# The first half of the next mixer pass as a stream beside the last chunk's delta rule

## The chip, the core and the metric

The kernel runs on one core of a Trainium2 chip. The metric is the device time of one execution in microseconds. Lower is better. The engines are TensorE (PE; its weight loads are listed apart as PEld), VectorE (DVE), ScalarE (ACT), GpSimd (POOL) and SyncE (SP), which here only issues transfers.

## The reference

One layer over 1024 tokens of width 1024, in float32. The mixer's input projection feeds two groups of heads, and its output goes through cross attention and a layer of experts.

```python
h = rmsnorm(x)
qkv, z, a_in, b_in, xr, gate = split(h @ w_in)
q, k, v = split(silu(causal_dwconv(qkv)))          # 4 taps along the tokens
g    = -exp(a_log) * softplus(a_in + dt_bias)
beta = sigmoid(b_in)
# gated delta rule, 4 heads of 128:
#   S_t = exp(g_t) S_{t-1} (I - beta_t k_t k_t^T) + beta_t v_t k_t^T,  o_t = S_t q_t
y_gdn = rmsnorm(o) * silu(z)
y_lru = rg_lru(causal_dwconv(xr)) * gelu(gate)     # a linear recurrence along the tokens
x = x + concat(y_gdn, y_lru) @ w_out
x = x + cross_attention(rmsnorm(x), rmsnorm(mem))  # 4 heads, 256 memory tokens
# experts: per token and each of 8 heads the 16 best of 128 x 128 product keys
x = x + sum_e gate_e * v_e * gelu(u_e . rmsnorm(x))
out = rmsnorm(x)
```

## The kernel before

The tokens go through the mixer in four passes of 256 (`T`), each of two chunks of 128 (`NB` = 2). `mixer` (L414) does a pass:

- It transposes the normed x into `hT`, multiplies for the gates g and beta, and then makes 12 tiles of 128 columns for query, key and value (`proj_T`, L319, with a weight tile of 512 KB each), each followed by a convolution on ScalarE and VectorE (`conv`, L415). They are kept in `qkv`: columns 0 to 3 are queries, 4 to 7 keys, 8 to 11 values. Columns 4 to 11 also hold the x of the next pass once keys and values are done with.
- It starts a stream `side` (L472): the z projection, and the linear recurrence with its eight projection tiles.
- It runs the gated delta rule chunk by chunk. A chunk is one long chain: small products on TensorE, each followed by a copy or a product on ScalarE or VectorE, six levels of a block recursion among them. In the last chunk, when keys and values are read, it issues the load of the next pass's x (`load_x`, L607).
- When the recurrence and both chunks are through, it norms the next x in place (`norm_x`, L738), and multiplies by the output projection (`out`, L523), which takes the x of the pass plus that product as `x1`.

Only then does the next pass begin. The passes run in the loop of `mixed` (L1224).

Beside them runs `attended` (L1238): first the keys and values of the memory, then the attention units (128, 128, 256, 256 and 256 tokens; `attend`, L757). A unit needs the `x1` of its tokens. It ends with the product keys, 16 tiles of queries and a search for the 16 best on VectorE, and with `choose` (L846), a stream that selects the experts. After the mixer comes the stream `gated` (L1233) that writes a table of gates for the 512 tokens that go by all experts, and at the end the dense part (`dense`, L1016), TensorE work for these tokens. The other 512 tokens go by their experts' rows: 1024 steps (`step`, L1138), each a gather of 128 rows by GpSimd, issued a few steps ahead, and one VectorE instruction over 128 x 1024 that is pinned behind the VectorE instruction emitted before it. Half of the steps of a block use the u rows, the others the v rows. The steps that are left after the dense part are emitted behind it.

The order in which all this is emitted is made by a planner in the program (`together`, L1176). It holds an estimate of when each engine is through. Of the streams that are ready it takes the one of least rank, and at equal rank the one that had the least TensorE time for its share:

```python
c = min(ready, key=lambda x: (x.rank, x.had / x.share))
```

The mixer and its side have rank 1 and share 6. `attended` has rank 2 and share 1 until the memory's keys and values are made, then rank 0 until the first experts are chosen, then rank 1. The gates have rank 0. A stream that yields `None` lets another go first.

The steps of the row stream are put between TensorE's instructions, one for each `pe.pace` nanoseconds of TensorE's estimated time (`tick`, L115):

```python
while self.ns > self.pace and (not self.real or dve.at < self.at + SLACK and not late_row()):
    self.ns -= self.pace
    step()
```

The pace is 2800 in the first three passes, 3500 in the fourth and in the gates (`PACES`, `PACE_G`), 2250 in the dense part (`PACE_D`). `mixed` sets it when a pass begins. The tiles `X1` (x1), `hT`, `qkv` and the memory that row gathers share with the first pass's split operands exist once.

Of the kernel before, what the change touches and what calls it, by code (L numbers as in the profile page):

```python
# [22 lines left out]
D0 = T                      # the tokens that go by all experts; the others go by their experts' rows  # L23
# [26 lines left out]
def block_kernel(ctx: ExitStack, tc: tile.TileContext, a):  # L50
# [3 lines left out]
    written = {}                # by tile: when which part of it is written, by the estimate  # L54
# [17 lines left out]
    class Engine:  # L72
        """An engine, and an estimate of when it is through with what it got so far."""
# [25 lines left out]
    class Paced(Engine):  # L99
        """The tensor engine, with steps of the stream of rows put between its instructions."""  # L100
# [29 lines left out]
    early = gat.tile([128, NROW + 2, D], FR, name="rb")   # until the rows come  # L130
# [9 lines left out]
    # ---------------------------------------------------------------- constants  # L140
    identf = consts.tile([128, 128], F, name="identf")
    identb = fc.tile([128, 128], BF, name="identb")
    triu = fc.tile([128, 128], F, name="triu")          # [t, i] = t <= i
    ones = fc.tile([128, 128], F, name="ones")
    negm = fc.tile([128, 128], BF, name="negm")         # [j, i] = -1e30 where i < j
    iota16 = consts.tile([128, 16], BF, name="iota16")
    # masks of the block recursion: W = (T X) o (I - M_s); M_s[r, c] = 1 where r // s is odd
    # and c // s = r // s - 1 (the first one transposed)
# [53 lines left out]
    lpar = ld("lpar", (128, 4, 4))                          # conv_b, ba, bx, lambda  # L202
# [9 lines left out]
    # ---------------------------------------------------------------- helpers  # L212
    def rsqrt(v, n, name):
        """1/sqrt(v) for a positive [128, n] tile: a bit guess and Newton's steps."""
# [11 lines left out]
    def softplus(x, n, name):  # L226
        """max(x, 0) + log1p(exp(-|x|)), the log by its atanh series."""
# [24 lines left out]
    def wload(src):  # L252
        """A piece of weights: 1024 rows x 128 columns, [128, 8, 128]."""
        w = wp.tile([128, D], F, name="w", bufs=3)
        sp.dma_start(w, src)
        return c8(w)

    def norm(X, nb, Y, junk):
        """RMS of token-major tiles, to Y."""
# [9 lines left out]
    class Both:  # L269
        """Two tiles [128, 4, T] as one of 8."""  # L270
# [6 lines left out]
    class Pair:  # L277
        """A float32 operand as two float32r parts, for the time in which the gathered rows' memory
        is free; tmp: a place for [128, T] of products."""
# [3 lines left out]
    def low(i):  # L283
        """Memory of the rows, [128, 8, T]."""
        return early[:, 2 * i:2 * i + 2, :].rearrange("p s (c t) -> p (s c) t", c=D // T)

    def transposed(hT, Y, nb, wcol):
        """Token-major tiles to [d, chunk, tok], by the weights."""
# [30 lines left out]
    def proj_T(wname, j, hT, n):  # L319
        """[128 columns, n tokens] of the product with one 128-column tile of weights."""  # L320
# [17 lines left out]
    def proj(wname, j, lhs, nb, b0=0):  # L338
        """The token-major products [128 tokens, nb blocks, 128 columns]."""
# [18 lines left out]
    # ---------------------------------------------------------------- once: masks, gates' constants  # L358
# [18 lines left out]
    # ---------------------------------------------------------------- once: memory keys, values  # L377
# [26 lines left out]
    # ---------------------------------------------------------------- the mixer, T tokens  # L404
# [9 lines left out]
    def mixer(fp, t0, qkv):  # L414
        def conv(ps, ti, w, out, bias=0.0):  # L415
            """Causal 4-tap convolution along the tokens of one channel tile."""
# [10 lines left out]

        hT = fp.tile([128, 8, T], F, name="hT", bufs=1)
        if t0 < EARLY:
            hT = Pair(hT, low(0), tmp)  # L430
        yield from transposed(hT, blocks_of(qkv[:, 4:12, :]), NB, wmixc)

        # a, b: token-major
# [25 lines left out]
        # q, k, v: channel-major, convolved, silu  # L459
        for j in range(12):  # L460
# [9 lines left out]
        ready = set()  # L470

        def side():  # L472
            # z: token-major, 2 silu(z)
# [8 lines left out]
            # RG-LRU: channel-major  # L482
# [252 lines left out]
        while not ready >= {"y", *range(NB)}:  # L735
            yield None
# [594 lines left out]
```

## Time and profile before

| | |
|---|---|
| Time, median of 3 runs | 3305.86 us (3297.55 to 3307.26) |
| Span of the profiled execution | 3300.7 us |
| TensorE busy | 3053.8 us, 93% |
| VectorE busy | 2740.9 us, 83% |
| ScalarE busy | 1282.9 us, 39% |
| GpSimd busy | 1430.2 us, 43% |
| Mean granted clock of TensorE | 0.962 |

The profile is one execution; its span runs from the first to the last instruction. Of its own time no other number than the span is given, so it stands 5.2 us below the median of the runs. Times in the rows count from the span's start. A matmul in float32 is two instructions in the trace. The granted clock is a share of 2.4 GHz; the other level, 1.2 GHz, shows as 0.50. The stages below are cut where the timeline shows the first products of a chunk, of an output projection or of a pass: the second pass's chunks begin at 406 and 542 us, its output projection at 640; the third pass begins at 676, its chunks at 728 and 866; the fourth pass's chunks begin at 1066 and 1207; the mixer ends near 1359, the gates run to 1821, the dense part to 3287.

### The profile page before, as it was taken

The page shows a single profiled execution, that of the slowest core. Times are in us where ns is not written, and L with a number is a line of the kernel's source. Part 1 is how long each engine was busy: PE and PEld are TensorE (multiplying, and loading weights), DVE is VectorE, ACT ScalarE, POOL GpSimd, SP SyncE. Part 2 cuts the span into 40 slices and gives each one's busy share as a digit, 9 for nine tenths or more (in the row PEclk, how much of TensorE's full clock was granted, in tenths as well). Part 3 has the DMA queues.
Part 4 walks back from the last instruction along what each step waited for, and adds up shares of the span by engine and source line. Part 5 has one row for each costly group of instructions (what it writes and reads, how often), then busy time and mean ns, then how long its engine had stood idle before and what let it go on. Part 6 is the DMA issues. An engine that isn't in the chain of part 4 may idle for free.

```text
span 3300.7 us, 46517 instructions
## 1 busy us (share of the span) xinstructions
PE 3053.8 (93%) x16212; PEld 2638.8 (80%) x16212; DVE 2740.9 (83%) x5999; ACT 1282.9 (39%) x2694; POOL 1430.2 (43%) x1045
## 2 busy tenths in 40 slices
PE   7999997698999989999868799999999999999998
PEld 6888887677988878898868677888888878888886
DVE  7634776877787889887899798888999988899998
ACT  6833452236323632465358332222222222222222
POOL 0000233334433343333333475665666665656663
PEclk9999998899999999999868899999999999999999
DMA  4346778688887678778888788999998999899995
GB/s 170 111 145 210 251 279 309 228 290 291 297 298 284 232 259 320 270 265 282 303 279 234 289 326 328 335 335 335 336 333 323 331 337 332 325 345 327 340 333 197
DMA packets 321547, 941.66 MB, mean 285 GB/s; under 512 B 28912, under 2 KB 108832, under 8 KB 319264
## 3 DMA queue, kind: packets, MB, share of 16 engines
q0 software_dynamic: 148048, 538.04, 46.2%
q1 hardware_dynamic: 107216, 367.08, 30.5%
q10 hardware_dynamic: 66048, 33.56, 3.6%
q8 instruction: 128, 2.10, 0.2%
q14 instruction: 107, 0.88, 0.1%
HBM read 894.53 MB, written 44.04 MB: 284 GB/s over the span
## 4 chain that ended last, share of the span: by engine, by line
PE 56%; DVE 14%; DMA 10%; issue 9%; POOL 7%; ACT 4%; SPq 0%; POOLq 0%; ACTq 0%; DVEq 0%
PE pj L106 17%; PE dh L106 15%; PE po L106 14%; PE gd L106 7%; POOL rb L1130 7%; DVE rb L82 4%; DMA rb<-in_u,idx 4%; DVE oh L82 2%; PE sc L106 1%; DMA w<-in_pwq 1%; PE tp L111 1%; DMA gd<-stage 1%; DMA w<-in_wout 1%; DVE cy L82 1%; ACT L82 1%
## 5 line engine op out<-in xcount | busy, mean ns | idle before, releaser
L1130 POOL DMA_INDIRECT rb<-in_u,idx x512 | 682.3, 1333 | 1128.2 <-DVE rb L82 509.6
L1130 POOL DMA_INDIRECT rb<-in_v,idx x512 | 739.1, 1444 | 702.8 <-DVE rb L82 487.8
L82 DVE SCALAR_TENSOR_TENSOR rb<-rb 128x1024 f32<-128x1024 f32 x512 | 614.4, 1220 | 97.8 <-DMA rb<-in_u,idx 97.5
L82 DVE SCALAR_TENSOR_TENSOR rb<-rb,ga 128x1024 f32<-128x1024 f32 x512 | 655.6, 1280 | 12.5 <-DMA rb<-in_v,idx 6.1
L106 PE MATMUL pj<-hT,w 128*128 128x256 f32 (+1 forms) x2880 | 592.5, 358 | 18.0 <-DMA w<-in_pwq 12.8
L106 PEld LDWEIGHTS pj<-hT,w 128*128 128x128 f32 x2880 | 493.9, 196 | 75.8 <-DMA w<-in_pwq 13.7
L106 PE MATMUL dh<-hT_h,uh 128*128 128x512 f32 x1024 | 407.5, 398 | 17.8 <-ACT dg L82 17.1
L106 PE MATMUL po<-vh,dah 128*128 128x512 f32 x1024 | 404.7, 395 | 8.9 <-DVE acc L82 7.6
L106 PE MATMUL dh<-hT_l,uh 128*128 128x512 f32 x1024 | 406.4, 397 | 0.0
L106 PE MATMUL dh<-hT_h,ul 128*128 128x512 f32 x1024 | 406.3, 397 | 0.0
L106 PE MATMUL po<-vh,dal 128*128 128x512 f32 x1024 | 405.1, 396 | 0.4 <-DVE dal L82 0.4
L106 PE MATMUL po<-vl,dah 128*128 128x512 f32 x1024 | 405.1, 396 | 0.0
L82 ACT CAST uh<-ur 128x1024 fp32r<-128x1024 f32 x128 | 134.7, 1052 | 551.8 <-PE dh L106 363.5
L106 PE MATMUL gd<-ohg,oh 128*128 128x128 f32 x1024 | 254.7, 409 | 47.2 <-ACT ohg L82 28.6
L106 PEld LDWEIGHTS gd<-ohg,oh 128*128 128x128 f32 x1024 | 245.9, 328 | 56.3 <-ACT ohg L82 42.1
L106 PEld LDWEIGHTS dh<-hT_h,uh 128*128 128x128 f32 x1024 | 193.4, 189 | 65.8 <-ACT dg L82 18.0
L106 PEld LDWEIGHTS po<-vh,dah 128*128 128x128 f32 x1024 | 192.1, 188 | 57.8 <-DVE acc L82 9.3
L106 PEld LDWEIGHTS dh<-hT_h,ul 128*128 128x128 f32 x1024 | 193.1, 189 | 47.1
L106 PEld LDWEIGHTS dh<-hT_l,uh 128*128 128x128 f32 x1024 | 193.4, 189 | 46.5
L106 PEld LDWEIGHTS po<-vl,dah 128*128 128x128 f32 x1024 | 192.2, 188 | 47.2
L106 PEld LDWEIGHTS po<-vh,dal 128*128 128x128 f32 x1024 | 192.2, 188 | 47.0 <-DVE dal L82 0.8
L82 ACT CAST dah<-dg 128x512 fp32r<-128x512 f32 x128 | 79.5, 621 | 301.0 <-DVE dg L82 301.0
(338 smaller groups left out, 4836.2 us busy)
## 6 DMA issues: line engine op xcount, KB each, us to landing
ur<-in_ut SPq DMA_DIRECT2D x128, 512.0 KB
vr<-in_v SPq DMA_DIRECT2D x128, 512.0 KB
w<-in_wA SPq DMA_DIRECT2D x80, 512.0 KB
w<-in_pwq SPq DMA_DIRECT2D x80, 512.0 KB
gd<-stage ACTq DMA_DIRECT2D x32, 1024.0 KB
G<-gd SPq DMA_DIRECT2D x16, 2048.0 KB
w<-in_wout SPq DMA_DIRECT2D x40, 512.0 KB
w<-in_wq SPq DMA_DIRECT2D x40, 512.0 KB
```

What stands on the lines that cost most here:

```text
L82: r = call(*args, **kw)
L106: self.engine.matmul(out, l, r, **kw)
L111: self.engine.transpose(out, i, ident)
L1130: pool.indirect_dma_start(out=t, out_offset=None, in_=a[ph], in_offset=bass.IndirectOffsetOnAxis(ap=B["idx"][:, k:k + 1], axis=0))
```

## The change

`mixer` is cut into `heads` (norm of x, transposes, g and beta, the 12 tiles and the start of `side`) and `delta` (the delta rule and the output projection). `heads` of the next pass is started as a stream of the mixer's rank and share right behind the load of x in the last chunk. It first waits until the pass's recurrence is through, sets the pace of its pass, norms x (with `hT` as scratch in place of `zs`) and makes the key and value tiles; it makes the query tiles only when the output projection of the pass before is finished, because that reads the query columns as y. `delta` of the next pass follows its `heads`. Nothing that is computed changes. Lines of comments that the diff also drops are left out here.

```diff
-    def mixer(fp, t0, qkv):
+    class Pass:
+
+        def __init__(self, t0):
+            self.t0, self.ready, self.x1 = t0, set(), []
+
+        def finished(self):
+            return self.t0 in done and (self.t0 > 0 or 128 in done)
+
+    def heads(fp, P, prev, qkv):
+
+        t0, ready = P.t0, P.ready
+
...
+        while prev and "y" not in prev.ready:
+            yield None
+        pe.pace = PACES[t0 // T]
         hT = fp.tile([128, 8, T], F, name="hT", bufs=1)
+        if prev:
+            X = blocks_of(qkv[:, 4:12, :])
+            norm(X, NB, X, hT[:, 0:D // T, :].rearrange("p c t -> p (c t)"))
+            yield list(X)
         if t0 < EARLY:
             hT = Pair(hT, low(0), tmp)
         yield from transposed(hT, blocks_of(qkv[:, 4:12, :]), NB, wmixc)
...
-        for j in range(12):
+        for j in (4, 5, 6, 7, 8, 9, 10, 11, 0, 1, 2, 3):
+            while j == 0 and prev and not prev.finished():
+                yield None
             ps = yield from proj_T("wA", j, hT, T)
...
-        ready = set()
+        P.g, P.beta, P.zs, P.yl = g, beta, zs, yl
...
         yield Stream(side(), RANK[2], SHARE[2])
 
-        y, x1 = Both(qkv[:, 0:4, :], yl), []
+    def delta(fp, P, qkv, after):
+
+        t0, ready, x1 = P.t0, P.ready, P.x1
+        g, beta, zs, yl = P.g, P.beta, P.zs, P.yl
+        y = Both(qkv[:, 0:4, :], yl)
...
             if b == NB - 1 and t0 + T < S:
-                load_x(qkv, t0 + T)             # keys and values of this pass are done with
+                load_x(qkv, t0 + T)
+                yield Stream(after(), RANK[1], SHARE[0])
             yield L_STEP
...
-        while not ready >= {"y", *range(NB)}:
-            yield None
-        if t0 + T < S:
-            norm_x(fp, qkv)
         yield from out(0 if t0 else 1, NB)
-        while t0 not in done:
+        while not P.finished():
             yield None
...
     def mixed():
-        """The mixers, then the gates of the passes that take all experts."""
-        for i in range(NP):
-            pe.pace = PACES[i]
-            yield from mixer(fp, i * T, qkv)
+
+        def chain(i, prev):
+            P = Pass(i * T)
+            yield from heads(fp, P, prev, qkv)
+            yield from delta(fp, P, qkv, lambda: chain(i + 1, P))
+            if i == NP - 1:
+                over.add(0)
+
+        over = set()
+        yield Stream(chain(0, None), RANK[1], SHARE[0])
+        while not over:
+            yield None
         mix.close()
```

## Rows read from the trace of the kernel before

**Rows 1.** The page, its first part: busy time, share of the span, instructions.

```profile
PE 3053.8 (93%) x16212; PEld 2638.8 (80%) x16212; DVE 2740.9 (83%) x5999; ACT 1282.9 (39%) x2694; POOL 1430.2 (43%) x1045
```

**Rows 2.** Windows by stage: length, engines' busy time (instructions), granted clock, DMA share, GB/s.

```profile
406.00:542.00 136.00, 116.23 (x781) 106.99 (x780) 98.98 (x256) 72.71 (x190) 55.17 (x47) 0.92 0.82 289
542.00:640.00 98.00, 67.98 (x504) 64.60 (x502) 80.67 (x320) 19.77 (x48) 26.16 (x25) 0.86 0.73 251
640.00:676.00 36.00, 28.38 (x209) 27.62 (x209) 24.15 (x58) 5.42 (x8) 17.95 (x15) 0.83 0.80 291
676.00:728.00 52.00, 50.98 (x239) 40.31 (x239) 41.24 (x122) 21.48 (x55) 15.22 (x15) 0.99 0.79 273
728.00:866.00 138.00, 127.86 (x769) 113.03 (x768) 106.95 (x233) 82.21 (x212) 59.67 (x51) 0.99 0.81 286
866.00:990.00 124.00, 115.28 (x767) 106.69 (x766) 99.31 (x305) 25.75 (x59) 49.85 (x43) 0.97 0.87 307
1066.00:1207.00 141.00, 126.94 (x752) 112.35 (x750) 122.54 (x393) 85.17 (x210) 50.76 (x41) 0.98 0.71 246
1207.00:1359.00 152.00, 141.27 (x1004) 131.68 (x1003) 128.24 (x432) 38.37 (x89) 59.06 (x50) 0.99 0.84 300
1821.00:3287.00 1466.00, 1439.67 (x6143) 1155.49 (x6144) 1324.66 (x1587) 421.23 (x534) 885.14 (x577) 0.99 0.89 324
```

**Rows 3.** Waits of TensorE from 542 to 676 us: total, times, longest.

```profile
PE tp L111 <- DVE go L82: 11.9, 1, 11.9
```

**Rows 4.** Windows, ten microseconds near the second pass's end.

```profile
630.00:640.00 10.00, 1.23 (x4) 0.73 (x4) 9.76 (x35) 2.13 (x5) 4.07 (x3) 0.50 0.49 158
```

**Rows 5.** Groups by line and shape, whole span: busy us, mean ns, idle before.

```profile
L82 DVE SCALAR_TENSOR_TENSOR cy<-cbuf,hcw,cy 128x256 f32<-128x256 f32 x144 | 69.5, 483 | 3.5 <-ACT cy L82 0.6 <-issue 0.2
L82 DVE SCALAR_TENSOR_TENSOR qkv<-cth,cy 128x256 f32<-128x256 f32 x48 | 20.3, 422 | 8.9 <-ACT cth L82 8.5 <-issue 0.3
...
L82 DVE COPY cbuf<-hist 128x3 f32<-128x3 f32 x64 | 10.9, 174 | 1.1
...
L82 ACT ACTIVATE zs<-qkv 128x1024 f32<-128x1024 f32 x8 | 8.4, 1054 | 10.2 <-DVE go L82 7.6 <-DMA qkv<-in_x 2.6
```

**Rows 6.** Row steps (u, v) from 340 to 1014, to 1821 and to 3301 us.

```profile
L82 DVE SCALAR_TENSOR_TENSOR rb<-rb 128x1024 f32<-128x1024 f32 x128 | 153.7, 1220 | 23.5 <-DMA rb<-in_u,idx 23.4
L82 DVE SCALAR_TENSOR_TENSOR rb<-rb,ga 128x1024 f32<-128x1024 f32 x84 | 107.2, 1277 | 4.9 <-DMA rb<-in_v,idx 4.2
...
L82 DVE SCALAR_TENSOR_TENSOR rb<-rb 128x1024 f32<-128x1024 f32 x128 | 153.9, 1218 | 18.9 <-DMA rb<-in_u,idx 18.7
L82 DVE SCALAR_TENSOR_TENSOR rb<-rb,ga 128x1024 f32<-128x1024 f32 x104 | 132.7, 1276 | 0.6 <-DMA rb<-in_v,idx 0.4
...
L82 DVE SCALAR_TENSOR_TENSOR rb<-rb,ga 128x1024 f32<-128x1024 f32 x325 | 416.9, 1283 | 6.9 <-DMA rb<-in_v,idx 1.6
L82 DVE SCALAR_TENSOR_TENSOR rb<-rb 128x1024 f32<-128x1024 f32 x256 | 306.8, 1221 | 55.4 <-DMA rb<-in_u,idx 55.3
```

**Rows 7.** Timeline of VectorE at the end: start us, us, what.

```profile
3272.52 2.60 DVE L82 SCALAR_TENSOR_TENSOR rb<-rb,ga 128x1024 f32<-128x1024 f32 x2
...
3280.40 1.29 DVE L82 SCALAR_TENSOR_TENSOR rb<-rb,f_y,wfin 128x1024 f32<-128x1024 f32 x1
...
3287.58 0.69 DVE L82 TENSOR_TENSOR acc<-acc,po 128x512 f32<-128x512 f32 x1
...
3295.65 1.28 DVE L82 SCALAR_TENSOR_TENSOR acc<-acc,f_y,wfin 128x1024 f32<-128x1024 f32 x1
```

**Rows 8.** Groups from 1815 to 1837 us, where row steps ran unpaced.

```profile
L1130 POOL DMA_INDIRECT rb<-in_v,idx x12 | 15.5, 1294 | 8.8 <-DVE rb L82 4.2 <-issue 1.8 <-DVE gate L82 1.7
L82 DVE SCALAR_TENSOR_TENSOR rb<-rb,ga 128x1024 f32<-128x1024 f32 x11 | 14.2, 1287 | 1.8 <-DMA rb<-in_v,idx 1.6
```

**Rows 9.** One line's instructions: ns min/median/max, first and last start us.

```profile
L106 PE MATMUL pj<-hT,rb x640: 276/280/682, 17.2 to 228.6; 128*128 128x256 f32 x160
...
L1130 POOL DMA_INDIRECT rb<-in_u,idx x512: 932/1145/3137, 361.9 to 2949.1; - x171
```

## The prediction

> **What bounds the kernel now.** I read the page first, then the windows cut at the stages, then the waits inside the emptiest stage, then the groups by line for the fetched rows, and last the timeline of the end.
>
> The page shows TensorE busy for 93% of the span [rows 1]. That is a mean over two halves with different limits. From 1821 us on, the products with all experts run, and TensorE is busy for 1439.7 of 1466 us [rows 2]: nothing in the mixer touches that. Before it lies the front, where the mixer passes, the attention units, the selections and the gates share the engines. The reader is to see in its windows that most stretches are fed: between 728 and 1359 us (the four windows that I call fed) TensorE idles 10.1 of 138, 8.7 of 124, 14.1 of 141 and 10.7 of 152 us, 44 of 555 or 8%. Two stretches are worse: 406 to 542 us idles 19.8 us, and 542 to 676 us, the last chunk of the second pass with its output projection, idles 30.0 + 7.6 = 37.6 us, at a granted clock of 0.86 and 0.83 [rows 2]. There the attention stream has run out of work, because the next unit needs the output of this pass, and the longest wait of TensorE is for the delta rule's own VectorE result, 11.9 us [rows 3].
>
> There is a second clock that sets the end. 1024 steps work on gathered rows. The planner doles them out by its estimate of TensorE's time: one per 2.8 us, 3.5 us from the fourth pass on, 2.25 us in the dense part. In the trace 212 steps lie between 361.9 us, where the first gather is issued [rows 9], and 1014, 232 between 1014 and 1821, 581 after [rows 6], that is one per 3.08, 3.48 and 2.50 us. The last of them ends at 3275.1 us, and TensorE's last result is added at 3287.6 [rows 7]. So the rows end with a slack of 12.5 us, 5 steps. A front that ends earlier hands out fewer steps, and those that remain are emitted behind the last instruction of the dense part.
>
> **The change part by part.** No arithmetic is removed or added, and no transfer: the norm, 16 transposes, the gates' products and the 12 projection tiles with their convolutions move, tile loads on SP's queue with them.
>
> 1. What moves beside the last chunk. One projection tile is 16 instructions; 239 of them fill 51.0 us in 676 to 728 us [rows 2], 0.213 us each, 3.4 us a tile. Eight key and value tiles make 27 us, the gates' products another 3.4, transposes some 3: 34 us of TensorE a pass, three times. Four query tiles (14 us) stay behind the output projection. In the third and fourth pass this only changes places with attention work, since 866 to 990 us is fed already.
>
> 2. What it fills. If 406 to 676 us came to the 8% of the fed stretches, the idle falls from 57.4 to 21.6 us: 35 us (rounded down). That is the value I take. Upper bound: the clock too. The granted clock means 0.92, 0.86 and 0.83 there against 0.98 in the fed windows, and (0.98 less these) times the busy 116.2, 68.0 and 28.4 us is 7 + 8 + 4 = 19 us: 54 in all. Lower bound: VectorE. It is busy 80.7 of 98 us in 542 to 640, and 9.76 of 10 us from 630 to 640, where TensorE has 1.23 us of work and the 1.2 GHz level of the clock (0.50) [rows 2, 4]. The move brings eight convolutions of three taps at 0.483, one product of 0.422 and two copies of about 0.17 us, 2.2 us each [rows 5], and the gates' small operations, 18 us and more, onto the engine that the chunk already waits for. If only what fits without delay counts, 17.3 us are free in 542 to 640 and part of it lies between dependent operations: 10 us.
>
> By the Trainium skill, "Perfetto Trace Analysis", Identifying the Most-Contended Engine, matmul busy time is a poor measure and the busy share of weight loads the better one. The rows disagree on what is free: in 676 to 728 us loads fill only 40.3 us, but the matmuls stand 0.213 us apart without a gap. By the loads the idle is 71 us in 406 to 676 us and 16% in the fed stretches, so 26 us would be filled in place of 35, and the total would come out 7 us later.
>
> 3. Rows that start later. The stream that makes the memory's keys and values has rank 2, the mixer rank 1. In the first pass the moved work is always ready and goes ahead of it. Memory products end at 228.6 us now [rows 9]; 34 us of work in front of them delays the first attention unit, its selection and so the first gather by 33 us, since TensorE was nearly full there. 33 / 3.08 = 10.7 steps are not handed out. Between nothing, if that unit catches up, and this; I take all of it, as its rank cannot be evaded.
>
> 4. The pace of 3.5 us now begins with the fourth pass's first half, that is with the last chunk of the third (866 us) and no longer at 1014, and earlier by the lead that the mixer has gained (33 + 35 us). 216 us at 3.48 in place of 3.08 us a step lose 216 x 0.0373 = 8.1 steps.
>
> 5. A front 35 us shorter hands out up to 35 / 3.48 = 10 steps fewer; none, if the planner's clock never contained that idle. Between 362 and 1014 us the planner counted 212 x 2.8 = 594 of 652 us, so it missed about half of the time in which TensorE idled or ran slow. I take 5.
>
> 6. What missing steps cost. 10.7 + 8.1 + 5 less the slack of 5 is 19 steps behind the end. They follow the last VectorE instruction of the dense part, which now ends at 3296.9 us; after them come the square, root and product that took from 3275.1 to 3281.7 us, and the 3.7 us until the span ends [rows 7]: 6.5 us more than now, plus the steps. Where the pace let go, 11 steps stand in 22 us, the instruction on VectorE at 1.29 us and the gather on GpSimd at 1.29 and 1.8 / 12 = 0.15 us to issue [rows 8]. VectorE alone bounds a step by 1.29 us from below, that burst with all between it by 2.0 from above; I take 1.4, near GpSimd's own rate. 19 steps are 26.6 us, the give-back 33 us.
>
> 7. At nothing: the x load (it was issued at the same place before), the order of key, value and query tiles, the norm's other scratch tile. Their cover is the same as before, except under the third rival.
>
> Sum: the saving F less the give-back. With F free, the missing steps are 12.5 + 0.18 F, and the change of the time is 24 - 0.75 F. At F = 35 it is -2 us. The profiled execution has a span of 3300.7 us, 5.2 below the runs' median of 3305.9; 3298.5 plus this is 3304 us. Measurement can tell about 0.3%, 10 us, from no change.
>
> **The rivals.**
>
> Forecast, no change that can be told: F between 19 and 45 us. The fed windows, and 57 us of idle in reach, speak for it; chance 0.36, range 3295 to 3315.
>
> Faster: the gain reaches the clock as well, F = 54, change -16 us: 3290. The low clock stands only where TensorE starved [rows 2], which speaks for it. The same time results if the first rows come no later (10.7 steps, 15 us, are not lost: 3289). Against both speak VectorE's load and the ranks. Chance 0.32, from F = 45 on.
>
> Slower: VectorE is what the last chunk waits for. The convolutions lengthen the delta rule's chain instead of filling its holes; F = 10, the steps are lost all the same, +16 us: 3322. For it speak the 9.76 of 10 us [rows 4] and that wait [rows 3]; against it that the selection which fills VectorE there would move later along with the attention. It decides below F = 19. Chance 0.22.
>
> Slower too: the norm of x now stands on ScalarE right behind the load's issue. Up to now those squares waited 2.6 us in all for x [rows 5]. Two blocks are 1.05 MB; at the 251 GB/s of 542 to 640 us [rows 2] that is 4 us alone and 8 with half of it. Seven us in three passes would hold up the copies of the delta rule queued behind, F = 14: +13 us, 3319. Chance 0.10. Beside it stands the Trainium skill, "TensorE: Matmul & The Clock Gate", Architectural detail: VectorE and ScalarE take their queue strictly in order. The wait of 2.6 us neither bears that out nor speaks against it.
>
> That the change does nothing (the first half never overlaps, because the recurrence of the pass isn't through) I give no chance of its own: the recurrence's condition is met ahead of every last chunk in the timeline.
>
> **Numbers.** Faster 0.32, same 0.36, slower 0.32. Eight in ten reach from 3282 (F = 54 and half of the late rows not lost) to 3326.
>
> **What would show it.** Step 1: tiles of the next pass's keys between the delta rule's products of a last chunk. Step 2: the dense part begins near 1786 us, the stretch of the second pass's end at over 0.9 busy. Step 3: the memory products end near 260 and the first gather stands near 395 us. Steps 4 to 6: about 420 steps ahead of the dense part, and a block of some 19 row steps behind the last addition of the dense part. Wrong it would be if the front keeps its 1821 us, if the rows still end inside the dense part, or if VectorE's waits in the last chunks grow.

## The result and the profile after

| | before | after |
|---|---|---|
| median of the runs compared (4 and 4) | 3306.56 us | 3336.03 us |
| span of the profiled execution | 3300.7 us | 3328.8 us |
| products of the memory end | 228.6 us | 273.2 us |
| first gather of rows | 361.9 us | 426.3 us |
| dense part begins | 1821.0 us | 1789.1 us |
| row steps ahead of it, in it, behind it | 444, 581, 0 | 400, 585, 40 |
| last addition of the dense part | 3287.6 us | 3253.1 us |
| from there to the end of the span | 13.1 us | 75.7 us |

The changed kernel is slower by 0.9%: ratio 1.0088, with a 95% interval of [1.0064, 1.0112]. Between the two profiles the 28.1 us split into 31.9 us less in front of the dense part, 2.6 us less in it, and 62.6 us more behind it.

The page's busy times have hardly moved against [rows 1]:

```profile
PE 3046.5 (92%) x16212; PEld 2631.4 (79%) x16212; DVE 2741.3 (82%) x5999; ACT 1284.8 (39%) x2694; POOL 1406.4 (42%) x1045
```

What moved is shown by PE's timeline of the changed kernel inside the last chunk of the second pass. Between the products of the recursion (gd) now stand whole projection tiles of the third pass (pj<-hT,w, 128 x 256):

```profile
559.75 0.94 PE L106 MATMUL gd<-Xi,TT 128*128 128x128 f32 x7
560.53 3.62 PE L106 MATMUL pj<-hT,w 128*128 128x256 f32 x16
563.99 1.05 PE L106 MATMUL gd<-W,Y 128*128 128x128 f32 x8
564.88 3.62 PE L106 MATMUL pj<-hT,w 128*128 128x256 f32 x16
```

The windows of the changed kernel, columns as in [rows 2]. The first two hold the end of the second pass's delta rule and its output projection, the next four stretches of the third and fourth pass, then the dense part and what follows it:

```profile
520.00:640.00 120.00, 106.97 (x725) 95.09 (x723) 95.94 (x324) 38.65 (x103) 38.43 (x35) 0.93 0.85 296
640.00:682.00 42.00, 41.05 (x289) 38.80 (x289) 34.15 (x140) 6.89 (x13) 13.64 (x12) 0.96 0.77 269
682.00:852.00 170.00, 153.22 (x961) 137.26 (x960) 127.64 (x328) 89.62 (x220) 72.65 (x60) 0.96 0.80 281
852.00:975.00 123.00, 116.98 (x689) 102.50 (x687) 98.84 (x326) 40.60 (x98) 34.84 (x31) 0.99 0.79 263
1020.00:1161.00 141.00, 127.92 (x757) 113.53 (x756) 124.69 (x439) 81.31 (x198) 50.79 (x39) 0.99 0.69 236
1161.00:1325.00 164.00, 147.36 (x1031) 137.06 (x1030) 132.41 (x394) 34.55 (x77) 63.54 (x54) 0.95 0.84 297
1789.00:3253.00 1464.00, 1442.37 (x6144) 1157.65 (x6144) 1324.94 (x1574) 419.82 (x532) 876.26 (x587) 0.99 0.91 327
3253.00:3329.00 76.00, 0.00 (x0) 0.00 (x0) 64.37 (x105) 3.45 (x6) 39.04 (x34) 0.52 0.76 277
```

The hole of [rows 2] is filled: 14.0 us of idle in these 162 us, where 542 to 676 us had 37.6 us in 134, and the clock there is 0.93 and 0.96 for 0.86 and 0.83. TensorE's longest wait there is no longer for VectorE as in [rows 3], but for ScalarE:

```profile
PE tp L111 <- ACT hT L82: 5.2, 2, 4.9
PE tp L111 <- ACT qkv L82: 2.5, 2, 1.9
PE tp L111 <- DVE go L82: 1.9, 1, 1.9
```

The four later stretches idle 52.5 of 598 us, 9%, where the fed windows of before had 8%. And 76 us at the end have no product at all. VectorE's timeline there, against [rows 7]:

```profile
3253.14 0.68 DVE L82 TENSOR_TENSOR acc<-acc,po 128x512 f32<-128x512 f32 x1
...
3262.97 1.28 DVE L82 SCALAR_TENSOR_TENSOR acc<-acc,f_y,wfin 128x1024 f32<-128x1024 f32 x1
3264.17 10.52 DVE L82 SCALAR_TENSOR_TENSOR rb<-rb,ga 128x1024 f32<-128x1024 f32 x8
3275.26 3.92 DVE L82 SCALAR_TENSOR_TENSOR rb<-rb,ga 128x1024 f32<-128x1024 f32 x3 [0.56 <-DMA rb<-in_v,idx]
...
3309.36 10.53 DVE L82 SCALAR_TENSOR_TENSOR rb<-rb,ga 128x1024 f32<-128x1024 f32 x8 [1.33 <-DMA rb<-in_v,idx]
...
3323.42 1.28 DVE L82 SCALAR_TENSOR_TENSOR rb<-rb,f_y,wfin 128x1024 f32<-128x1024 f32 x1
```

From 3264.17 to 3319.89 us stand 39 row steps, 1.43 us each, and one before them. The numbers of steps are read from VectorE's groups, in front of the dense part (u and v rows) and behind it, against [rows 6]:

```profile
L82 DVE SCALAR_TENSOR_TENSOR rb<-rb 128x1024 f32<-128x1024 f32 x256 | 306.3, 1217 | 40.3 <-DMA rb<-in_u,idx 38.7 <-issue 1.7
L82 DVE SCALAR_TENSOR_TENSOR rb<-rb,ga 128x1024 f32<-128x1024 f32 x144 | 183.9, 1277 | 1.9 <-DMA rb<-in_v,idx 1.0
...
L82 DVE SCALAR_TENSOR_TENSOR rb<-rb,ga 128x1024 f32<-128x1024 f32 x40 | 51.4, 1284 | 5.6 <-DMA rb<-in_v,idx 4.5
```

The memory and the first gather, against [rows 9] (line L1151 was L1130):

```profile
L106 PE MATMUL pj<-hT,rb x640: 275/280/579, 16.5 to 273.2; 128*128 128x256 f32 x160
...
L1151 POOL DMA_INDIRECT rb<-in_u,idx x512: 932/1146/3097, 426.3 to 3026.3; - x171
```

### The profile page after: what moved, and what is told of

Same layout as the page of the kernel before. It is cut to its first block, busy times and chain, and to the rows that moved or that the text cites. A ratio compares the mean times of both kernels' runs of the same rounds, so it can differ in the third digit from the quotient of the medians.

```text
span 3328.8 us, 46501 instructions
## 1 busy us (share of the span) xinstructions
PE 3046.5 (92%) x16212; PEld 2631.4 (79%) x16212; DVE 2741.3 (82%) x5999; ACT 1284.8 (39%) x2694; POOL 1406.4 (42%) x1045
## 4 chain that ended last, share of the span: by engine, by line
PE 69%; DVE 14%; DMA 8%; ACT 4%; issue 4%; POOL 1%; SPq 0%; ACTq 0%; POOLq 0%; DVEq 0%
PE dh L106 21%; PE po L106 20%; PE pj L106 17%; PE gd L106 8%; DVE rb L82 4%; DMA rb<-in_u,idx 2%; PE sc L106 2%; PE tp L111 2%; DVE oh L82 1%; DMA w<-in_pwq 1%; DMA gd<-stage 1%; POOL rb L1151 1%; ACT L82 1%; DMA w<-in_wo 1%; DVE cy L82 1%
## 5 line engine op out<-in xcount | busy, mean ns | idle before, releaser
L1151 POOL DMA_INDIRECT rb<-in_u,idx x512 | 666.4, 1302 | 1231.2 <-DVE rb L82 579.7
L1151 POOL DMA_INDIRECT rb<-in_v,idx x512 | 731.2, 1428 | 672.3 <-DVE rb L82 443.8
```

The lines of the kernel that those rows point to most:

```text
L1151: pool.indirect_dma_start(out=t, out_offset=None, in_=a[ph], in_offset=bass.IndirectOffsetOnAxis(ap=B["idx"][:, k:k + 1], axis=0))
```

## The experiments

Two theories stood against each other. **A**: the front's 32 us are a gain of their own, and the steps that it no longer hands out can be won back. **B**: the front is shorter because it does 44 steps fewer; at equal numbers of steps it is as long as before. In the table the steps are counted in VectorE's rows, and the front ends with the first product of the dense part, in one profile of each kernel. Executions of one kernel spread by 5 to 26 us in total time, and the experiments ran on several chips; how far the front's end alone varies was not measured. So differences of single profiles under 10 us are not read, and those up to 20 only where several agree.

| kernel | steps in front | front ends, us | steps behind | ratio to before |
|---|---|---|---|---|
| before | 444 | 1821.0 | 0 | |
| after | 400 | 1789.1 | 40 | 1.0088 [1.0064, 1.0112] |
| e1 after, memory first | 414 | 1802.2 | 24 | 1.0036 [1.0020, 1.0053] |
| e2 after, pace at the delta rule | 410 | 1801.4 | 28 | 1.0049 [1.0032, 1.0066] |
| e3 after, shorter pace in the dense part | 400 | 1790.9 | 0 | 1.0009 [0.9999, 1.0019] |
| e4 before, third pass at 3.5 us | 415 | 1809.2 | 23 | 1.0043 [1.0028, 1.0057] |
| e5 after, shorter paces in front | 459 | 1829.4 | 0 | 1.0052 [1.0035, 1.0069] |
| e6 before, longer paces in front | 377 | 1758.1 | 61 | 1.0074 [1.0051, 1.0097] |
| e7 after, memory first, pace late and shorter | 448 | 1826.1 | 0 | 1.0035 [1.0008, 1.0061] |
| e8 after, only the third pass's heads early | 440 | 1850.8 | 0 | 1.0142 [1.0111, 1.0172] |
| e16 after, longer paces in front | 364 | 1759.1 | 74 | one run, 3360.8 us |

### Winning the steps back: e1 to e3, and the same loss without the change: e4

```diff
# e1
-        while prev and "y" not in prev.ready:
+        while prev and ("y" not in prev.ready or first.rank == 2):
# e2: out of heads, to the begin of delta
-        pe.pace = PACES[t0 // T]
# e3
-PACE_G, PACE_D = 3500.0, 2250.0
+PACE_G, PACE_D = 3500.0, 2080.0
# e4, in the kernel before
-PACES = (2800.0, 2800.0, 2800.0, 3500.0)
+PACES = (2800.0, 2800.0, 3500.0, 3500.0)
```

> The changed kernel, but heads of the second pass waits until the memory's keys and values are through. Theory (the moved work of the first pass goes ahead of the memory stream, so the first rows come 64 us later, and the steps not handed out follow the dense part at 1.43 us each): the memory products end near 230 us again, the first gather stands between 360 and 375 us, 18 to 20 steps are regained, some 20 are left behind the dense part, and the time falls by 25 to 30 us against the changed kernel, to 3306 to 3311. Rival (the attention units are slowed by the mixer's extra pieces wherever these stand, not by the rank): the first gather stays later than 400 us and the time within 8 us of the changed kernel's 3336.

> The changed kernel, but the pace of a pass is set where its delta rule begins and not where its heads begin, so 3.5 us rules from about 973 us and not from about 858. Theory (each step that is not handed out ahead of the dense part costs 1.43 us behind it): 115 us at 2.8 in place of 3.5 hand out 8 steps more, 31 are left behind the dense part, the time falls by 11 us, to 3325. Rival (the pace is not what limits the steps there, since they are held back by the estimate of VectorE): within 4 us of the changed kernel's 3336.

> The changed kernel with a pace of 2.08 us in place of 2.25 in the dense part: room for 635 steps there in place of 587, so that none is left behind it. Theory (the tail of 39 steps is the whole give-back and the front's 34 us are real): the dense part begins near 1789 us as before, TensorE ends near 3255, the span near 3267, the run near 3273. Rival (VectorE, busy for 1325 of 1464 us there, has no room for 48 more instructions of 1.28 us, 61 us): TensorE waits for it, the dense part grows by 20 us or more and the time is 3290 or above.

> The kernel before with the third pass at 3.5 us in place of 2.8, and no other change. Theory (steps that are not handed out in the front are paid behind the dense part): 338 us at that pace lose 13 to 22 steps, the slack of 5 takes some, 8 to 17 follow the dense part, and the time rises by 6.5 us and 1.4 us for each, by 18 to 30 us to 3324 to 3336. Rival (a front with fewer row steps is itself faster, since VectorE is freed of them): the front shortens by as much, and the time stays within 5 us of 3306.

With the memory first (e1) its products end at 230.5 us, and 14 steps come back; with the late pace (e2) 10 do. The front ends 13 and 12 us later for it. e1 stayed short of its theory: 18 to 20 steps and 3306 to 3311 us were expected, the median is 3319 us, and the first gather, at 391.9 us, is still 30 us late. e2 came out as expected (3324.5 us). In e3 no step is left behind, but the dense part takes 1501 us in place of 1464, and the time is 3309 us and not 3273, as the rival had it: 40 steps more in it cost 0.94 us each, though TensorE idled for only 21 of the 1464 us there. e4 takes 29 steps from the front of the kernel before, more than expected, and the front ends 12 us earlier, without any of the change; its time, 3322 us, lies under the 3324 to 3336 of its theory.

### The number of steps alone: e5 and e6; all the mending together: e7; one pass alone: e8

```diff
# e5, after               # e6, before               # e7, after with e1, e2
+PACES = (2520.0, 2520.0, 2520.0, 3150.0)   # e5; PACE_G 3150
+PACES = (3110.0, 3110.0, 3110.0, 3890.0)   # e6; PACE_G 3890
+PACES = (2675.0, 2675.0, 2675.0, 3340.0)   # e7; PACE_G 3340
# e8, after with e2
+        while prev and ("y" not in prev.ready or prev.t0 != T and not prev.finished()):
```

> The changed kernel with all paces of the front at nine tenths (2520 and 3150), so that about 444 steps stand ahead of the dense part, as in the kernel before, and none behind it. Theory A (the front's 32 us are idle that the change filled; the steps cost the front little): the front ends near 1805, the time is 3287 to 3295. Theory B (most of the 32 us are the 44 steps that the front no longer does, at 0.4 to 1.2 us each): the front ends between 1810 and 1835, the time is 3298 to 3320.

> The kernel before with all paces of the front longer by a ninth (3110 and 3890), so that about 400 steps stand ahead of the dense part, as in the changed kernel. Theory A: the front stays within 6 us of 1821, some 40 steps follow the dense part, and the time is 3306 + 6.5 + 57, near 3365. Theory B: the front shortens by 44 times 0.4 us or more, to 1803 or less, and the time is 3350 or less; what then is left between 1789 and its front is the change's own saving.

> The changed kernel with heads waiting for the memory's products, the pace set where a delta rule begins, and the front's paces shorter by 4.5% (2675 and 3340): 440 steps or more ahead of the dense part, none behind it. Theory A: the front near 1805, time 3287 to 3295. Theory B: front 1812 to 1830, time 3297 to 3315.

> The changed kernel, but only the third pass's heads run beside the second pass's last chunk; those of the second and fourth pass wait until the pass before is finished; pace set where a delta rule begins. Theory (all that can be filled is the idle of 406 to 676 us, most of it in the second pass's last chunk, and the memory stream is left alone): first gather near 362 to 375 us, 430 steps or more ahead of the dense part, TensorE over 0.88 busy in the second pass's last chunk, front 1805 to 1815, time 3295 to 3303. Rival (the idle there returns elsewhere, since VectorE sets the pace of that stretch): front 1818 or later, time 3305 or above.

e6 speaks for B most clearly. The kernel before, with 67 steps fewer in front, has a front 63 us shorter, 0.94 us a step and twice the 32 us of the change:

```profile
L82 DVE SCALAR_TENSOR_TENSOR rb<-rb 128x1024 f32<-128x1024 f32 x249 | 300.2, 1217 | 30.4 <-DMA rb<-in_u,idx 30.3
L82 DVE SCALAR_TENSOR_TENSOR rb<-rb,ga 128x1024 f32<-128x1024 f32 x128 | 163.4, 1277 | 3.8 <-DMA rb<-in_v,idx 2.7
...
L106 PE MATMUL dh<-hT_h,uh x1024: 389/396/628, 1758.1 to 3203.3; 128*128 128x512 f32 x171
```

On a straight line between e4 (415 steps) and e6 (377) it would end near 1789 us at 400 steps, just where the changed kernel ends. e7 has as many steps in front as the kernel before (448 and 444) and none behind; its front ends 5 us later and its total is longer, not shorter. e1 and e4 (414 and 415 steps) differ by 7 us. e5 and e6 lie within the bounds of B, and e7 at their edge (3316 us for at most 3315).

e8 fits neither theory: at 440 steps its front ends 30 us later than before. TensorE idles there for 234 us in place of 207. Its longest new wait, 14.6 us up to 1038 us, stands between the third pass's output projection and the fourth pass's heads. There ScalarE and VectorE norm x for the next attention unit and for the held-back pass at the same time, while the kernel before norms the pass's x ahead of the output projection. Where the rest of the 30 us comes from is not settled. No version in the table beats the kernel before; e3 comes nearest.

Where the filled hole went is seen in the windows of the kernel before and of e7, both cut where an attention unit begins. Before:

```profile
234.00:354.00 120.00, 111.01 (x872) 102.22 (x872) 62.66 (x328) 42.02 (x117) 0.00 (x0) 0.99 0.59 198
354.00:780.00 426.00, 358.81 (x2298) 323.96 (x2297) 323.87 (x964) 171.25 (x443) 152.14 (x135) 0.93 0.79 279
780.00:1152.00 372.00, 349.43 (x2171) 314.04 (x2170) 296.67 (x782) 155.35 (x375) 142.31 (x119) 0.98 0.79 279
1152.00:1398.00 246.00, 225.78 (x1437) 207.43 (x1436) 214.18 (x787) 91.53 (x228) 89.59 (x76) 0.98 0.81 285
1398.00:1821.00 423.00, 371.03 (x1756) 349.11 (x1755) 368.99 (x1096) 253.94 (x693) 153.42 (x120) 0.87 0.84 272
```

And e7:

```profile
237.00:397.00 160.00, 144.34 (x1004) 129.58 (x1005) 85.26 (x398) 52.56 (x151) 4.42 (x5) 0.97 0.56 183
397.00:757.00 360.00, 315.33 (x2131) 287.73 (x2131) 280.20 (x851) 149.82 (x396) 133.59 (x114) 0.94 0.81 287
757.00:1141.00 384.00, 353.13 (x2176) 317.09 (x2177) 302.96 (x806) 161.12 (x381) 159.04 (x129) 0.96 0.82 286
1141.00:1404.00 263.00, 224.79 (x1386) 203.41 (x1385) 223.69 (x838) 76.12 (x186) 98.88 (x85) 0.92 0.80 275
1404.00:1826.00 422.00, 380.84 (x1816) 360.36 (x1814) 372.55 (x1061) 270.12 (x736) 167.75 (x124) 0.90 0.87 282
```

TensorE's idle (length less the first busy time) is 9.0, 67.2, 22.6, 20.2 and 52.0 us before, 15.7, 44.7, 30.9, 38.2 and 41.2 us in e7. The second pass's stretch gives up 22 us of idle. The one before it and the two behind it take 33 us, the last gives 11: 171.0 and 170.7 in all. In the whole front TensorE idles for 207 us in both. The hole was not filled for good; it moved.

### What a step costs, and what the change is worth without steps: e9 to e18

e9 and e10 hand out next to no steps in front, so most follow the dense part and only the front's end is read, that is the start of the dense part's first product (dh). e11, e12, e14 and e15 let the VectorE instruction of a step work on 64 of its 1024 columns, with gathers and plan as they were; e17 and e18 shrink the gathers too.

```diff
# e9 (before), e10 (after), e13 (e10 with e1)
+PACES = (1.0e9, 1.0e9, 1.0e9, 1.0e9)       # PACE_G too
+        pe.pace, pe.real, pe.ns = PACE_D, False, 0.0
# e11 (before), e12 (after); the same for the product with B["a"]
+                dve.engine.scalar_tensor_tensor(t[:, 0:64], t[:, 0:64], 1.0, B["h"][:, 0:64], op0=OP.mult, op1=OP.mult,
+                                                accum_out=B["hd"][:, k:k + 1]))
+            dve.spend([t, t, B["h"], B["hd"][:, k:k + 1]])
# e14 (e12), e15 (e11), e16 (after)
+PACES = (2600.0, 2600.0, 2600.0, 3250.0)   # e14; PACE_G 3250
+PACES = (3110.0, 3110.0, 3110.0, 3890.0)   # e15; PACE_G 3890
+PACES = (3000.0, 3000.0, 3000.0, 3750.0)   # e16; PACE_G 3750
# e17 (e11), e18 (e12)
-            out=t, out_offset=None, in_=a[ph],
+            out=t[:, 0:64], out_offset=None, in_=a[ph].rearrange("n (c d) -> (n c) d", d=64),
```

> The kernel before, with a pace so long that no row step is handed out ahead of the dense part; nearly all of those 444 steps then follow behind the dense part, so the total grows by some 440 x 1.43 less 0 = 600 us and only the start of the dense part (dh) is read from it, against the same edit of the kernel after. Theory B (the VectorE steps of the rows stand in the idle that the moved projections were to fill, so each costs the front 0.7 to 0.94 us): the dense part begins 310 to 420 us ahead of 1821, at 1400 to 1510, because 444 steps by 0.7 to 0.94 us go. Rival (TensorE bounds the front and the steps cost it next to nothing, the differences between the runs so far have another cause): above 1700 us.

> The same edit of the kernel after; again only the start of the dense part (dh) is read. Theory B1 (without rows VectorE has room, so the moved projections do fill the idle of the second pass's end): it begins 20 to 50 us earlier than with the kernel before and no rows. Rival B2 (the moved work costs as much elsewhere, in the attention that it delays, whatever the rows do): the two begin within 10 us of each other.

> The kernel before with row steps whose VectorE instruction works on 64 of the 1024 columns; the dot products and sums over the other 960 columns are left out, the gathers and the plan stay as they are. Read is the start of the dense part, 1821 us before. If VectorE's time is what a step costs the front: about 440 steps by 0.7 to 0.94 us less, 1400 to 1510 us, no more than what no rows at all give. If the gather (DMA or GpSimd) is the cost: it stays above 1750.

> The kernel after with the same short row steps (960 of 1024 columns of each left out, the gathers and the plan as they are); the start of the dense part is read, 1789 us after. Theory B1: with VectorE relieved the change saves its idle, so the dense part begins 20 to 50 us earlier than in the kernel before with short steps, and more than the 44 steps' gathers could explain. Rival B2: within 10 us of it.

> The kernel after without row steps ahead of the dense part, and the next pass's heads wait until the memory's keys and values are made. Only the start of the dense part is read: 1672.8 with the kernel before without rows, 1702.9 with the kernel after without rows. Theory: the 30 us are the memory's late start (its products end at 276.5 in place of 227.9); then it begins between 1665 and 1685. Rival: the cost lies in the later passes, where the heads stand in front of attention work that is due; then it begins above 1692.

> The kernel after with short row steps (960 of 1024 columns of each left out) at paces of 2.6 and 3.25 us, so that some 435 to 450 of them stand ahead of the dense part, as with the kernel before and short steps (442, dense part from 1786.2). Theory: with VectorE relieved the change does save its idle; 1741.5 plus some 45 steps at 0.26 us, 1750 to 1760. Rival: the 45 us were the steps not handed out, at 0.9 us each or more as with full steps; 1778 to 1790.

> The kernel before with short row steps (960 of 1024 columns left out) and the longer paces of the run with few rows, so that some 375 of them stand ahead of the dense part in place of 442. Theory: a step costs the front mostly VectorE's time, so short steps cost 0.26 us or less each; the dense part begins at 1765 to 1775. Rival: what a step costs is its place in the plan and its gather; then it begins near 1786 less 65 by 0.94, 1720 to 1740.

> The kernel after, full steps, with longer paces (3.0 and 3.75 us), so that some 375 to 380 steps stand ahead of the dense part, as with the kernel before and few rows (377, dense part from 1758.1). Theory: at equal numbers of steps the change saves nothing here either; 1755 to 1775. Rival: the change saves its 30 us where VectorE has fewer steps; below 1740. About 62 to 65 steps then follow the dense part, so the total is near 3330.

> The kernel before with short row steps and short gathers: each gather brings 128 pieces of 64 columns (32 KB in place of 512 KB) from other places of the tables, the VectorE instruction works on those 64 columns, and the plan is as it was. The sums over the other 960 columns are left out. Read is the start of the dense part: 1821.0 with full steps, 1786.2 with short steps and full gathers, 1672.8 with no steps. Theory: the gathers' transfer, which holds up VectorE's ordered queue, is most of the other 113 us; then 1675 to 1710. Rival: it is the order in which the plan with rows emits the streams; then 1760 to 1790.

> The kernel after with the same short steps and short gathers (960 of 1024 columns of each left out, the plan as it is). The dense part starts at 1789.1 with full steps, 1741.5 with short steps and full gathers, 1702.9 with no steps. Theory, transfer: 1700 to 1720, some 20 to 30 us behind the kernel before with the same edit, as with no steps. Rival, the plan's order: 1725 to 1745, and still ahead of the kernel before by some 40 us.

| steps | before: steps in front, its end | after: steps in front, its end |
|---|---|---|
| full | 444, 1821.0 us | 400, 1789.1 us |
| short on VectorE | 442, 1786.2 us; e15: 377, 1722.8 us | 398, 1741.5 us; e14: 440, 1763.9 us |
| short, and short gathers | 442, 1726.0 us | 398, 1706.0 us |
| none | 4, 1672.8 us | 4, 1702.9 us; e13: 4, 1688.1 us |

Both expectations for steps removed altogether fell. The kernel before loses 148 us to 440 steps, 0.34 us on the mean and not 0.7 to 0.94: the last 67 cost 0.94 each (e6), the 373 below them 0.23. The windows of the whole front, before, after and e9, show what such a loss is made of:

```profile
0.00:1821.00 1821.00, 1613.56 (x10069) 1483.23 (x10069) 1406.41 (x4365) 859.40 (x2157) 545.07 (x469) 0.94 0.74 255
0.00:1789.10 1789.10, 1604.16 (x10068) 1473.76 (x10068) 1352.11 (x4322) 861.60 (x2157) 491.11 (x425) 0.95 0.73 247
0.00:1672.80 1672.80, 1571.01 (x10069) 1457.68 (x10069) 912.50 (x3654) 852.14 (x2148) 19.53 (x31) 0.98 0.43 138
```

Of the 148 us, 106 are idle time of TensorE (207 us before, 102 in e9). The other 42 are busy time for the same products, at a granted clock of 0.94 with steps and 0.98 without. The 32 us of the change split likewise, into 22.5 of idle and 9.4 of busy time.

And without steps the change makes the front 30 us longer, where B said that with VectorE relieved it would pay. The windows to the second attention unit, to the third, and to the dense part show where. e9:

```profile
0.00:357.00 357.00, 310.01 (x2414) 289.61 (x2414) 203.12 (x739) 187.37 (x421) 7.59 (x20) 0.97 0.48 159
357.00:707.00 350.00, 334.90 (x2286) 306.25 (x2285) 188.16 (x709) 166.38 (x438) 8.11 (x8) 0.98 0.44 149
707.00:1673.00 966.00, 926.30 (x5374) 862.03 (x5373) 521.42 (x2207) 498.59 (x1290) 3.84 (x3) 0.98 0.40 126
```

e10:

```profile
0.00:394.00 394.00, 346.29 (x2579) 319.66 (x2579) 210.45 (x735) 198.38 (x459) 7.61 (x20) 0.97 0.48 157
394.00:746.00 352.00, 332.53 (x2326) 304.56 (x2327) 178.56 (x689) 181.33 (x457) 7.95 (x8) 0.98 0.42 141
746.00:1703.00 957.00, 905.26 (x5165) 838.88 (x5165) 519.71 (x2234) 474.04 (x1235) 3.84 (x3) 0.96 0.40 125
```

In e9 the stretch from the second unit to the third idles 15 us, not the 67 of the kernel before: without steps there is no hole to fill. The change then puts the second unit off by 37 us, loses 2 more up to the third, and gets 9 back in the rest. Putting the memory first (e13) takes away half of the 30 us, between its two expectations; the other half is within the spread of single profiles and stays open.

e11 fell to its rival: its front is 35 us shorter and not 310 or more, so VectorE's work on the columns is not what most of a step costs. For the kernel before the 148 us split into three, in the order in which they were taken away: 35 us go with VectorE's own work on the columns (e11), 60 us more with the bytes of the gathers (e17), and 53 us are left that belong to the plan with steps in it, to the issue of the gathers and to all that is not bytes or columns. In the changed kernel they are 48, 35 and 3 us for 398 steps. These are differences of single profiles, and another order could give other shares. So for the kernel before neither the transfer nor the plan's order is the whole cost, and the expectations of e17 (from either side) missed; e18 came out where the transfer puts it, but 20 us ahead of e17 and not behind it.

The gathers' bytes show in VectorE's waits for them up to the dense part. With full steps VectorE waits for the u rows for 42 us ([rows 6]), with short ones for 81, so part of what e17 gives back is a wait that full steps do not have. The first line is e11, the second e17:

```profile
DVE rb L1150 <- DMA rb<-in_u,idx: 81.1, 25, 9.0
```

```profile
DVE rb L1150 <- DMA rb<-in_u,idx: 38.0, 20, 3.7
```

How such a wait reaches TensorE is seen in one place of the kernel before, inside the stretch of 542 to 676 us. VectorE waits 4.10 and 1.17 us for gathered rows; behind these steps stands its addition of a product of the output projection to `X`, and TensorE waits 5.37 us for that addition:

```profile
668.40 1.23 DVE L82 SCALAR_TENSOR_TENSOR rb<-rb 128x1024 f32<-128x1024 f32 x1 [4.10 <-DMA rb<-in_u,idx]
670.81 1.23 DVE L82 SCALAR_TENSOR_TENSOR rb<-rb 128x1024 f32<-128x1024 f32 x1 [1.17 <-DMA rb<-in_u,idx]
...
671.96 0.41 DVE L82 TENSOR_TENSOR X<-X,pj 128x256 f32<-128x256 f32 x1
...
672.43 2.08 PE L106 MATMUL pj<-w,qkv 128*128 128x128 f32 x8 [5.37 <-DVE X L82]
```

How much of the 60 us takes this way no run shows. It is not the only way: TensorE's own waits for transfers fall as well, from 27.8 us in e11 to 5.3 in e17, most of them for tiles of weights, as those of the output projection (e11, then e17):

```profile
PE pj L106 <- DMA w<-in_wout: 7.5, 6, 2.2
```

```profile
PE pj L106 <- DMA w<-in_wout: 2.2, 4, 0.7
```

The waits of TensorE that VectorE ends fall by about as much, from 75 to 49 us. Another 13 us are busy time, at a granted clock of 0.96 for 0.95.

e15 came out as its rival had it, which agrees that the columns are not the main cost: with short steps too, 65 steps fewer end the front 63 us earlier. e12 begins its dense part 45 us ahead of e11, as B1 had it for VectorE relieved, but with 44 steps fewer. With as many of them (e14 and e11) 22 us are left, from one profile each: a saving at most, when steps are cheap but present, and a little less than the theory of e14 had. In the whole time e11 and e12 come to 0.9869 [0.9827, 0.9911] and 0.9858 [0.9820, 0.9895] of the kernel before. With full steps no pair of equal numbers shows a saving: 7 us for it (e1 and e4), 5 against (e7 and before). At few steps (e16 and e6) it is 1 us against it with 13 steps fewer. e16's front lies where its theory had it; its total came out at 3361 and not near 3330, with 74 steps behind.

## Why the prediction was wrong

By its own sum, step by step:

1. What moves: right; the tiles stand between the products of the last chunk, as shown.
2. What it fills: 35 us forecast, 32 us measured in the front's end. That the number came near is luck, for the reason failed. The step said that 35 us of idle are saved whatever the row steps do. At 448 steps (e7) the idle is as long as before, only in later stretches. The clock did rise in the filled stretch, as the bound of 54 us had it; the mean of the execution still went from 0.962 to 0.957, with 0.52 behind the dense part. By the Trainium skill, "Perfetto Trace Analysis", Identifying the Most-Contended Engine, TensorE's headroom is judged by its rate of useful work or by the busy share of its weight loads, and not by the busy time of its matmuls. The prediction's estimate by the loads was 26 us. No run at an equal number of full steps bears out 26 us or 35, and neither busy share told that the stretch has no hole without row steps (e9).
3. Rows that start later: right in kind, too small. The memory's products end 44.6 us later, not 33, and the first gather stands 64.4 us later: 64.4 / 3.08 = 21 steps in place of 10.7. The first unit's selection comes 56 us later (the 16 best at 387 us in place of 331), and its first gather another 9. The memory's rank, which the step named, is about half of it: with the memory first (e1) the gather is still 30 us late, and only with the second pass's heads held back (e8, 367.5 us) does most of that go. The heads stand in front of the first unit itself too, which takes 160 us in e7 and 120 before.
4. The pace: 8.1 steps forecast, 6 to 10 measured (e2 gives 10 back, with a front 12 us longer that hands out about 4 of them).
5. The shorter front: 5 steps forecast; 32 / 3.48 = 9 by the measured front. With 21 and 6 to 10 that makes 36 to 40 of the 44 steps that are missing; the rest was not traced. Four of the 44 found room in the dense part, as the slack of 5 had it.
6. What missing steps cost: 1.43 us each, as forecast (1.4), but 40 of them and not 19. With the finish the give-back is 62.6 us against 33. This is the term that was mis-sized, because twice as many steps are missing, the late rows (step 3) above all: -35 + 33 became -34.5 + 62.6.
7. The load of x shows as 7.3 us of ScalarE's waits, see the last rival; a cost of the scratch tile was not looked for.

Beneath the mis-sized term lies the error that the experiments found: steps were taken as free wherever TensorE has work. By e6 and e3 they cost 0.94 us each in the front above some 377 of them and 0.94 us each in the dense part above some 585, so a saving in the front and steps not done there cannot be booked apart. That is why winning the steps back (e1, e2, e5, e7) or doing them in the dense part (e3) returned at best to the time before, and never to the 35 us below it.

The rivals. The one nearest in time, 3322 us by VectorE, had the wrong mechanism: the delta rule's wait for VectorE in the last chunk fell from 11.9 to 1.9 us, and the hole was filled. The idle came back in other stretches, and there no run separates VectorE from the attention that the moved work puts off. The faster case did not occur. The norm of x on ScalarE was a small matter: its squares waited 7.3 us for the load in three passes, against 2.3 for those that are left in the old place, not 7 us in each pass:

```profile
L82 ACT ACTIVATE hT<-qkv 128x1024 f32<-128x1024 f32 x6 | 6.3, 1055 | 7.5 <-DMA qkv<-in_x 7.3 <-PE pj L106 0.3
...
L82 ACT ACTIVATE zs<-qkv 128x1024 f32<-128x1024 f32 x2 | 2.1, 1057 | 2.3 <-DMA qkv<-in_x 2.3
```

Of the signs, the dense part began near 1786 us (1789.1) and the stretch was over 0.9 busy or near it (0.89 and 0.98); the memory, the first gather and the two numbers of steps missed as above. Of the signs of being wrong, neither a front that keeps its 1821 us nor rows that still end inside the dense part came; no sign stood for more missing steps than forecast.

## What to carry to other kernels

Where a planner doles out side work by the estimated time of the main work, a shorter stretch also does less of it: compare two kernels at equal amounts of side work before calling the difference a saving. Price the side work in every place by changing its amount in the kernel before, which here took two lines (e6) and shows that 67 steps are worth 63 us. A hole is a saving only if the work that made it (here the row steps) does not dig it again later: take that work out once and see whether the hole is there without it, as e9 did.

## What was not expected of the hardware

The cost of one row step (a 512 KB gather and 1.28 us of VectorE) depends on where it stands, though VectorE is busy for only 1406 of the 1821 us of the front: 0.23 us each for the first 373 in the front, 0.94 each for the next 67, 0.94 each in the dense part above 585 (where TensorE is busy for 1442 of 1464 us), 1.43 behind everything. All but the last are differences of single profiles. Cutting the columns to a sixteenth moved the front by 35 us, cutting the bytes as well by 60 us more, with TensorE's own waits for transfers down from 27.8 to 5.3 us. The bytes also weigh on the dense part, which took 1460 and 1452 us from its first to its last product in e11 and e12 and 1440 us in both e17 and e18, at a DMA share of 0.42 in place of 0.89 and 0.90.
